# Left-over dots of the last stage in the ring's slots, and a denser, longer list of dots before it

## The chip, the cores and the metric

One core of a Trainium2 chip runs the kernel, with its engines PE (TensorE, matmuls), DVE (VectorE), ACT (ScalarE), POOL (GpSimd, which here issues the gathers) and SP (SyncE, which issues the plain loads). The metric is the device time of one execution in microseconds. Lower is better.

## The reference, cut to what matters

The layer mixes 512 tokens of width 1024 (RG-LRU and gated linear attention heads) and then sends each token through a PEER expert mixer. The change touches only the mixer:

```python
def _peer(u, w_q, keys, u_tab, v_tab):
    ...
    top_s, pos = lax.top_k(cand_s, PEER_TOPK)              # 16 of 16384 experts in each of 8 heads
    expert = jnp.take_along_axis(cand_e, pos, axis=-1)
    weight = jax.nn.softmax(top_s, axis=-1).astype(u.dtype)
    ...
    def block(args):
        xb, eb, wb = args
        act = jax.nn.gelu(jnp.einsum("td,tkd->tk", xb, u_tab[eb]), approximate=False) * wb
        return jnp.einsum("tk,tkd->td", act, v_tab[eb])
```

Each token thus needs 128 dots of its vector u with rows of `peer_u`, and a sum of 128 rows of `peer_v` weighted by the gelu of those dots.

## The kernel before

The 512 tokens are four tiles of 128: t0, t1 (gathered) and d0, d1 (dense). A gathered tile takes each of its 128 selections by an indirect DMA that brings one row of a table for each of the 128 tokens (512 KB, `gather`, L909), issued by POOL. For `peer_u` a DVE instruction multiplies the rows with the tokens' vectors and adds up along the row (a dot, `u_fin`, L923). For `peer_v` a DVE instruction adds the weighted rows to `y` (`v_row`, L976). The dense tiles multiply with the whole of both tables on PE instead, block by block of 128 rows, 128 blocks in each table.

The mixer runs in three stages.

- Scores, 402 to 910 us: `d_scores` (L1024) for blocks b = 0 to 127 of `peer_u`, loaded by SP as `ut_s` three blocks ahead into the four slots "mid". Beside it DVE makes the selections (`select`) and dots of t0, then t1. The program's order here is written by a loop (L1219 to L1233) that runs at build time over two lists, `pe_list` and `dve_list`, each with a clock made up of estimates: a block of scores counts 3.45. Whenever the second clock has reached `due`, the loop writes a dot (`row_u`), adds 1.32 to that clock and PACE to `due`. It stops when "end" is in `done`, which `pe_list` sets after block 121 (L1174). "sel" is set at block 100, once both selections of the dense tiles have been turned. The order on ACT, PE, DVE and POOL is that of the list (`manual_schedule`, L1151); nothing ties a dot to a block of scores but the slots and rows it needs.
- Middle stage, 910 to 1120 us: the loop at L1242. It builds, from one-hot products, the weights of the dense tiles into A, and adds up `peer_v` rows of t0 on PE (`v_load_pairs`, `v_pairs`). In 14 of its 32 rounds it also starts a dot of t1 (L1254). PE, ACT and DVE keep the written order (PIN); POOL's order is chosen by the scheduler.
- Last stage, 1120 to 1607 us: the loop at L1280 over the 128 blocks of `peer_v`, loaded as `vt_s` four blocks ahead into "mid". For five blocks of six `v_split` (L1067) splits weights and values into high and low parts: ACT casts `gh` and `vh`, DVE subtracts to `gl` and `vl`, and `d_out` (L1081) runs three products on PE. Every sixth block runs unsplit. Beside it `rest` (L1266) works off what t1 still needs: for each head its left-over dots, then 16 rows of `v_row`. There are n_g = left-over dots + 128 such steps, spread over 124 blocks (L1289).

Slots matter here. `ring()` gives one of four slots of 128x1024 floats (RING, L41), used in turn. Tag `u_d` has two slots, which hold the dense tiles' vectors until the scores end; then `vl` takes them in turn. A dot's rows go where `u_start` (L914) says: into the ring, into `rz` for every third dot before "sel", and into `rw`, in tag `u_d`, once "u" is set, which is after the scores. Behind the last dot of a head `u_done` (L928) runs a gelu on ACT and a product on DVE.

Of the kernel before, what the change touches and what calls it, by code (L numbers as in the profile page):

```python
# [47 lines left out]
def tile_kernel(ctx, tc, x, cx, pos, ada_w, cols, rows, consts, w_in, wgate, w_g, w_out, w_q, keys_t,  # L48
# [219 lines left out]
    def load_in(c0):  # L268
        while todo and (c0 not in ready or len(ready) < AHEAD):
            c = todo.pop(0)  # L270
            ready[c] = load_one(c)
        return ready.pop(c0)
# [25 lines left out]
    w = load_in(2464)  # L298
# [325 lines left out]
    for n, k in enumerate((0, 1, 2, 3, 4, 5, 6, 7)):  # L624
        tag, nb = (("acc", 1) if n < 1 else ("wraw", 3) if n < 4 else ("whi", 2) if n < 6 else ("wlo", 2))
        w = wst.tile([128, D], F32, name="wo", tag=tag, bufs=nb)
# [19 lines left out]
    def wq_load(a):  # L646
        wq[a] = za.tile([128, KD, 128], F32, name="wq", bufs=4)
        SY.dma_start(wq[a], w_q[a])
# [21 lines left out]
    def ring(shape=(128, D), dt=F32):  # L670
        return B.tile(list(shape), dt, name="ring", tag="ring", bufs=RING)
# [10 lines left out]
    def prep_mm(t):  # L682
        xt, pt = xin[t]
        V.tensor_add(xt, xt, pt)
        for n in range(2):
            p = bank("pw")
            for k in range(KD):
                PE.matmul(p, mix_k(k)[:, t * 128:(t + 1) * 128], wo[k][:, n * 512:(n + 1) * 512],
                          start=(k == 0), stop=(k == KD - 1))
            V.tensor_mul(pt[:, n * 512:(n + 1) * 512], p, gate_mix[:, n * 512:(n + 1) * 512])  # L690
        V.tensor_add(xt, xt, pt)
        SY.dma_start(x1_d[t * 128:(t + 1) * 128, :], xt)
        ss = kb.tile([128, 1], F32, name="ss1", bufs=2)
        S.activation(pt, xt, AF.Square, accum_out=ss)
        r = rstd_of(kb, ss, 1, 1.0 / D)
        V.tensor_scalar(pt, xt, r[:, 0:1], None, op0=OP.mult)
# [4 lines left out]
    def prep_t(t):  # L701
        pt = xin[t][1]
        ut = [tok_u(t, k) for k in range(KD)]
        for h in range(2):
            p = bank("pt")
            for j in range(4):
                PE.transpose(p[:, j * 128:(j + 1) * 128], pt[:, (h * 4 + j) * 128:(h * 4 + j + 1) * 128], ident)
            for j in range(4):
                k = h * 4 + j
                if j % 2:  # L710
                    S.activation(ut[k], p[:, j * 128:(j + 1) * 128], AF.Identity,
                                 scale=a2[:, k:k + 1], bias=b2[:, k:k + 1])
                else:
                    V.tensor_scalar(ut[k], p[:, j * 128:(j + 1) * 128], a2[:, k:k + 1], b2[:, k:k + 1],
                                    op0=OP.mult, op1=OP.add)

    def prep_n(t):
        u_n[t] = B.tile([128, D], F32, name=f"u_n{t}")
        for h in range(2):
            p = bank("pu")  # L720
            for j in range(4):
                PE.transpose(p[:, j * 128:(j + 1) * 128], tok_u(t, h * 4 + j), ident)
            S.copy(u_n[t][:, h * 512:(h + 1) * 512], p)
# [4 lines left out]
    def q_mm(ts, h):  # L728
        p = bank("pq")
        for j in range(2):  # L730
            w = wq.pop(h * 2 + j)
            for k in range(KD):
                PE.matmul(p[:, j * 256:(j + 1) * 256], w[:, k], pair_u(ts, k), start=(k == 0), stop=(k == KD - 1))
        q = zq.tile([128, 2, 2, 128], F32, name="q", bufs=2)
        S.copy(q, p.rearrange("p (j t i) -> p j t i", j=2, t=2))
        return ts, h, q

    def s_mm(ts, h, q):
        p = bank("pss")
        for i, t in enumerate(ts):  # L740
            for j in range(2):
                c = (i * 2 + j) * 128
                PE.matmul(p[:, c:c + 128], q[:, j, i], kt[:, h * 2 + j, :], start=True, stop=True)
        for i, t in enumerate(ts):
            if (t, h // 4) not in ss_:
                ss_[t, h // 4] = s_slot([128, 8, 128], "s")
            S.copy(ss_[t, h // 4][:, h % 4 * 2:h % 4 * 2 + 2],
                   p[:, i * 256:(i + 1) * 256].rearrange("p (j t) -> p j t", j=2))
            done.add((t, h))
# [105 lines left out]
    def open_l():  # L855
        za_s.close()
        wst_s.close()
        lp = pool(ctx, "lp")
        L["st"] = [lp.tile([128, 2, 128], F32, name="sel_t", tag="st", bufs=4) for _ in range(4)]
        L["z"] = [lp.tile([128, 127], F32, name=f"z{i}") for i in range(8)]  # L860
        L["lp"] = lp
        for z in L["z"]:
            G.memset(z, 0.0)
        L["ix"] = lp.tile([128, 128], I32, name="ix")
        L["at"] = lp.tile([128, 128], F32, name="at")
        L["a"] = []
        open_a(0)
# [41 lines left out]
    def gather(tab, ix, g):  # L909
        G.indirect_dma_start(out=g, out_offset=None, in_=tab,  # L910
                             in_offset=bass.IndirectOffsetOnAxis(ap=ix, axis=0))
        return g

    def u_start(t, k):  # L914
        if "u" in done:
            g = B.tile([128, D], F32, name="rw", tag="u_d", bufs=2)
        elif "sel" not in done and k % 3 == 2:
            g = zs.tile([128, D], F32, name="rz", bufs=2)
        else:
            g = ring()  # L920
        return t, k, gather(peer_u, sel_i[t][:, k:k + 1], g)
# [183 lines left out]
    def row_u():  # L1105
        g = u_next(t0) or (not left[t0]["u"] and u_next(t1))
        if g:
            u_fin(*g)
        return g

    done = set()
# [7 lines left out]
    def pe_list():  # L1119
        prep_mm(t0)  # L1120
        prep_mm(t1)
        yield 28
        prep_mm(d0)
        prep_t(t0)
        prep_t(t1)
        yield 16
        between = {1: lambda: (prep_n(t0), prep_mm(d1)), 3: lambda: prep_t(d0), 4: lambda: prep_n(t1),
                   5: lambda: prep_t(d1)}
        last = None
        for h in range(NH):  # L1130
            for a in (h * 2 + 4, h * 2 + 5):
                if a < 16:
                    wq_load(a)
            q = q_mm(GT, h)
            if last:
                s_mm(*last)
            last = q
            if h in between:
                between[h]()
            yield 22.5 if h == 1 else 8.2  # L1140
        s_mm(*last)
        open_l()
        done.add("l")
        seq = [("u", 0), ("u", 1)]
        for h in range(NH):
            seq += [("w", 2 * h), ("w", 2 * h + 1)] + [("u", 4 * h + 2 + i) for i in range(4)]
        seq += [("u", b) for b in range(34, 128)]
        for n in range(3):
            u_load(*seq[n])
        last = None  # L1150
        region.enter_context(tc.manual_schedule(engines={ET.Activation, ET.PE, ET.DVE, ET.Pool}))  # L1151
        for n, (kind, b) in enumerate(seq):
            if n + 3 < len(seq):
                u_load(*seq[n + 3])
            if kind == "w":
                if b % 2:
                    if last:
                        s_mm(*last)
                    last = q_mm(DT, b // 2)
                    yield 8.1  # L1160
                continue
            if b == A_PARTS[1]:
                open_a(1)
            if b == A_PARTS[2]:
                while not all(("turn", t) in done for t in DT):
                    yield None
                done.add("sel")
                open_a(2)
            d_scores(b)
            if last and b == 34:  # L1170
                s_mm(*last)
                last = None
            yield 3.45
            if b == 121:  # L1174
                done.add("end")
        done.add("u")
        flush(True)
        region.close()
# [31 lines left out]
        while "end" not in done:  # L1210
            yield None

    PACE = 2.4
    due = 70.
    ET = mybir.EngineType
    region = ExitStack()
    clock = [0.0, 52.0]
    streams = [pe_list(), dve_list()]
    while streams[0] or streams[1]:  # L1219
        if "l" in done and "u" not in done:  # L1220
            flush()
        if "end" not in done and clock[1] >= due and clock[1] <= clock[0] + 4 and row_u():
            clock[1] += 1.32
            due = max(due + PACE, clock[1] - 6)
            continue
        i = 0 if streams[0] and (clock[0] <= clock[1] or not streams[1]) else 1
        c = next(streams[i], "end")
        if c == "end":
            streams[i] = None
        elif c is None:  # L1230
            clock[i] = clock[1 - i] + 0.1
        else:
            clock[i] += c  # L1233
# [4 lines left out]
    with tc.manual_schedule(engines=PIN):  # L1238
# [3 lines left out]
        for n in range(0, 64, 2):  # L1242
# [8 lines left out]
            if 2 <= n:  # L1251
                if late:
                    u_fin(*late.pop())
                g = n < 30 and u_next(t1)  # L1254
# [11 lines left out]
    def rest():  # L1266
        for h in range(NH):
# [3 lines left out]
            for _ in range(TOPK):  # L1271
                v_row(t1, left[t1]["v"].pop(0))
                yield

    n_g = len(left[t1]["u"]) + NSEL
    gath = rest()
    k = 0
# [91 lines left out]
```

## Time and profile before

| | |
|---|---|
| median of 3 runs | 1616.89 us (1609.41 to 1619.64) |
| profiled execution | 1608.13 us |
| its span | 1606.4 us |
| PE busy | 1486.4 us (93%) |
| DVE busy | 1193.9 us (74%) |
| POOL busy | 630.4 us (39%) |
| ACT busy | 527.1 us (33%) |
| HBM read | 477.69 MB |
| dots in `ring`, `rz`, `rw` | 159, 63, 34 |

The span runs from the first to the last instruction of the profiled execution. Busy shares are means over stages with different limits, so the stages have to be read one by one, by windows of time. PEclk is the granted clock of PE as a share of 2.4 GHz. The DMA share is the mean busy share of the core's 16 DMA engines; it can come out just over 1.

### The profile page before, as it was taken

Reading aid. Unit: us, or ns where it says so; the run is one execution under the profiler, and the core shown is the slowest. Engines: PE = TensorE matmul, PEld = TensorE weight load, DVE = VectorE, ACT = ScalarE, POOL = GpSimd, SP = SyncE. Lnnn points to the kernel's source line nnn. Section 1 sums busy time; section 2 is a strip of 40 time slices with the busy share of each in tenths; the row PEclk is TensorE's granted clock in tenths of the full one; section 3 lists DMA queues with packets and bytes.
Section 4 is the critical chain, followed back from the end, with each engine's and each line's share of the span. In section 5 each row is a group of like instructions: output and inputs, shape, how many; then the busy total and the mean of one; then the engine's idle time right before and its main releaser. Section 6 shows DMA issues by size and latency. Waiting matters only on the chain. (4 is left out here: it accounts for less than half of the span.)

```text
span 1606.4 us, 20273 instructions
## 1 busy us (share of the span) xinstructions
PE 1486.4 (93%) x6668; PEld 1103.9 (69%) x6668; DVE 1193.9 (74%) x3078; ACT 527.1 (33%) x1001; POOL 630.4 (39%) x579
## 2 busy tenths in 40 slices
PE   8899999999999999999999999999899999696585
PEld 2678778478888888888888744454566667474354
DVE  5889965429989979997964177666788889584467
ACT  3667874122111111111120144444333443232123
POOL 0111100005546646564544376664545555241230
PEclk9999999999999999999999999999999999897798
DMA  9655432448999989998999699999899999795575
GB/s 373 199 183 177 145 118 79 185 152 296 361 359 394 388 324 405 387 399 329 394 371 395 216 347 351 358 348 356 326 359 370 386 369 390 281 332 212 175 258 214
DMA packets 152569, 484.28 MB, mean 301 GB/s; under 512 B 14864, under 2 KB 36752, under 8 KB 152336
## 3 DMA queue, kind: packets, MB, share of 16 engines
q0 software_dynamic: 79072, 287.87, 48.6%
q1 hardware_dynamic: 73392, 195.13, 32.7%
q8 instruction: 52, 0.85, 0.2%
q14 instruction: 53, 0.43, 0.1%
HBM read 477.69 MB, written 5.24 MB: 301 GB/s over the span
## 5 line engine op out<-in xcount | busy, mean ns | idle before, releaser
L910 POOL DMA_INDIRECT ring<-in_dram,sel_i x287 | 363.6, 1267 | 374.8 <-DVE y L982 150.1
L1030 PE MATMUL pds<-u_d,ut_s 128*128 128x256 f32 x2048 | 444.8, 379 | 0.0
L1030 PEld LDWEIGHTS pds<-u_d,ut_s 128*128 128x128 f32 x2048 | 388.4, 190 | 52.5
L924 DVE SCALAR_TENSOR_TENSOR ring<-ring,u_n 128x1024 f32<-128x1024 f32 x159 | 191.8, 1219 | 35.4 <-DMA ring<-in_dram,sel_i 35.3
L1090 PE MATMUL ya<-vl,gh 128*128 128x512 f32 x428 | 146.1, 424 | 63.8 <-DVE vl L1078 63.0
L982 DVE SCALAR_TENSOR_TENSOR y<-ring,act,y 128x1024 f32<-128x1024 f32 x127 | 162.5, 1280 | 28.2 <-DMA ring<-in_dram,sel_i 27.4
L1090 PE MATMUL ya<-vh,gh 128*128 128x512 f32 x428 | 147.5, 427 | 7.1 <-ACT vh L1076 7.1
L1090 PEld LDWEIGHTS ya<-vl,gh 128*128 128x128 f32 x428 | 81.5, 199 | 96.2 <-DVE vl L1078 79.3
L1090 PE MATMUL ya<-vh,gl 128*128 128x512 f32 x428 | 139.7, 409 | 0.0
L1078 DVE TENSOR_TENSOR vl<-vt_s,vh 128x1024 fp32r<-128x1024 f32 x107 | 132.7, 1240 | 9.0 <-ACT vh L1076 8.8
L1033 ACT ACTIVATE A<-pds 128x1024 f32<-128x1024 f32 x32 | 32.8, 1024 | 302.9 <-PE pds L1030 276.9
L1076 ACT CAST vh<-vt_s 128x1024 fp32r<-128x1024 f32 x107 | 112.3, 1049 | 59.3 <-DMA vt_s<-in_dram 47.0
L973 PE MATMUL yv<-ring_s,z 128*64 128x512 f32 x256 | 121.4, 603 | 5.9 <-DMA ring_s<-in_dram,ix 4.0
L973 PE MATMUL yv<-ring,z 128*64 128x512 f32 x256 | 121.5, 603 | 1.2 <-DMA ring<-in_dram,ix 0.7
L1075 ACT CAST gh<-A 128x256 fp32r<-128x256 f32 x107 | 43.4, 405 | 214.7 <-PE ya L1090 192.7
L1090 PEld LDWEIGHTS ya<-vh,gh 128*128 128x128 f32 x428 | 84.2, 198 | 36.9 <-ACT vh L1076 10.0
L910 POOL DMA_INDIRECT rz<-in_dram,sel_i x63 | 76.6, 1215 | 64.0 <-DVE rz L924 37.2
L1090 PEld LDWEIGHTS ya<-vh,gl 128*128 128x128 f32 x428 | 85.0, 199 | 21.1
L924 DVE SCALAR_TENSOR_TENSOR rw<-rw,u_n 128x1024 f32<-128x1024 f32 x34 | 41.6, 1224 | 73.5 <-DMA rw<-in_dram,sel_i 71.5
L1039 DVE TENSOR_TENSOR ab<-cst,sel_t 128x512 f32<-128x512 f32 x64 | 44.1, 689 | 58.7 <-PE pwb L1054 31.8
L910 POOL DMA_INDIRECT ring<-in_dram,ix x64 | 62.8, 982 | 47.9 <-PE pwb L1054 22.1
L910 POOL DMA_INDIRECT ring_s<-in_dram,ix x64 | 63.9, 998 | 44.4 <-DMA ut_s<-in_dram 20.8
(310 smaller groups left out, 2375.5 us busy)
## 6 DMA issues: line engine op xcount, KB each, us to landing
ut_s<-in_dram SPq DMA_DIRECT2D x144, 512.0 KB
vt_s<-in_dram SPq DMA_DIRECT2D x128, 512.0 KB
adw<-in_dram POOLq DMA_DIRECT2D x34, 512.0 KB
wraw<-in_dram SPq DMA_DIRECT2D x21, 512.0 KB
wada<-in_dram SPq DMA_DIRECT2D x16, 512.0 KB
wq<-in_dram SPq DMA_DIRECT2D x16, 512.0 KB
ring<-in_dram,sel_i POOLq DMA_INDIRECT x287
wo<-in_dram SPq DMA_DIRECT2D x8, 512.0 KB
```

The costliest lines, as they stand in the source:

```text
L910: G.indirect_dma_start(out=g, out_offset=None, in_=tab, in_offset=bass.IndirectOffsetOnAxis(ap=ix, axis=0))
L924: V.scalar_tensor_tensor(g, g, 1.0, u_n[t], op0=OP.mult, op1=OP.mult, accum_out=act[t][:, k:k + 1])
L973: PE.matmul(yv[0][h * 64:h * 64 + 64, n, :], z[:, 63 - i:127 - i], g[:, n * 512:(n + 1) * 512], start=(i == 0), stop=(i == 63), skip_group ...
L982: V.scalar_tensor_tensor(L["y"], g, a, L["y"], op0=OP.mult, op1=OP.add)
L1030: PE.matmul(p, ut[:, k], u_d[k // 4][:, k % 4].rearrange("p j t -> p (j t)"), start=(k == 0), stop=(k == KD - 1))
L1033: S.activation(a_of(b - 3, 4), ld["ps"].rearrange("p h n -> p (h n)"), AF.Gelu)
L1039: V.tensor_tensor(ab[:, 0], iota[:, None, :].to_broadcast([128, 4, 128]), st[0][:, j, n0:n0 + 4, None].to_broadcast([128, 4, 128]), op=OP. ...
L1075: S.copy(gh, a)
L1076: S.copy(vh, vt)
L1078: V.tensor_sub(vl, vt, vh.bitcast(F32))
L1090: PE.matmul(ya[t][:, n, :], g[:, j * 128:(j + 1) * 128], v[:, n * 512:(n + 1) * 512], start=(b == 0 and i == 0), stop=(b == 127 and i == l ...
```

## The change

Three edits. A dot started after the middle stage, marked by "w", takes its slot from the ring instead of `rw`. The build loop paces the dots by LATE = 2.2 instead of 2.4 once "sel" is set. "end", at which the loop writes no more dots, comes after block 124 instead of 121.

```diff
--- before.py
+++ after.py
@@ -912,7 +912,9 @@
         return g
 
     def u_start(t, k):
-        if "u" in done:
+        if "w" in done:
+            g = ring()
+        elif "u" in done:
             g = B.tile([128, D], F32, name="rw", tag="u_d", bufs=2)
         elif "sel" not in done and k % 3 == 2:
             g = zs.tile([128, D], F32, name="rz", bufs=2)
@@ -1171,7 +1173,7 @@
                 s_mm(*last)
                 last = None
             yield 3.45
-            if b == 121:
+            if b == 124:
                 done.add("end")
         done.add("u")
         flush(True)
@@ -1210,7 +1212,7 @@
         while "end" not in done:
             yield None
 
-    PACE = 2.4
+    PACE, LATE = 2.4, 2.2
     due = 70.
     ET = mybir.EngineType
     region = ExitStack()
@@ -1221,7 +1223,7 @@
             flush()
         if "end" not in done and clock[1] >= due and clock[1] <= clock[0] + 4 and row_u():
             clock[1] += 1.32
-            due = max(due + PACE, clock[1] - 6)
+            due = max(due + (LATE if "sel" in done else PACE), clock[1] - 6)
             continue
         i = 0 if streams[0] and (clock[0] <= clock[1] or not streams[1]) else 1
         c = next(streams[i], "end")
@@ -1272,6 +1274,7 @@
                 v_row(t1, left[t1]["v"].pop(0))
                 yield
 
+    done.add("w")
     n_g = len(left[t1]["u"]) + NSEL
     gath = rest()
     k = 0
```

## Rows read from the trace of the kernel before

**Rows 1.** the page, busy tenths of 40 slices of 40.16 us, granted clock, DMA share.

```profile
PE   8899999999999999999999999999899999696585
PEclk9999999999999999999999999999999999897798
DMA  9655432448999989998999699999899999795575
```

**Rows 2.** windows: length, busy us (instructions) of PE PEld DVE ACT POOL, PEclk, DMA, GB/s.

```profile
1160.00:1382.00 222.00, 212.95 (x825) 153.00 (x824) 196.90 (x207) 87.60 (x122) 110.66 (x87) 1.00 0.99 378
1382.00:1407.00 25.00, 12.40 (x35) 7.62 (x34) 9.73 (x15) 4.72 (x7) 4.61 (x4) 0.79 0.52 185
1448.50:1542.00 93.50, 54.14 (x155) 36.54 (x154) 37.81 (x56) 17.07 (x25) 16.07 (x16) 0.79 0.52 177
```

**Rows 3.** lines L1022 and L910 from 1160 to 1382; columns: ns min/median/max, first, last.

```profile
L1022 SPq DMA_DIRECT2D vt_s<-in_dram x73: 327/328/328, 1160.4 to 1381.0; - x73
...
L910 POOL DMA_INDIRECT ring<-in_dram,sel_i x87: 932/938/2014, 1159.2 to 1379.7; - x87
```

**Rows 4.** waits, 1448.5 to 1542; columns: us in total, times, longest us.

```profile
DVE rw L924 <- DMA rw<-in_dram,sel_i: 54.9, 15, 7.4
...
PE ya L1090 <- DVE vl L1078: 34.2, 10, 7.8
```

**Rows 5.** timeline of one dot; columns: start, us, instruction, idle before and releaser.

```profile
1458.50 0.94 POOL L910 DMA_INDIRECT rw<-in_dram,sel_i  x1 [6.19 <-DVE rw L924]
...
1459.81 1.22 PE L1090 MATMUL ya<-vl,gh 128*128 128x512 f32 x2 [7.79 <-DVE vl L1078]
...
1463.09 1.23 DVE L924 SCALAR_TENSOR_TENSOR rw<-rw,u_n 128x1024 f32<-128x1024 f32 x1 [3.34 <-DMA rw<-in_dram,sel_i]
```

**Rows 6.** timeline of POOL, first gathers of and after the two groups of dots.

```profile
1382.05 0.94 POOL L910 DMA_INDIRECT rw<-in_dram,sel_i  x1 [0.30 <-issue]
...
1407.02 2.01 POOL L910 DMA_INDIRECT ring<-in_dram,sel_i  x1 [9.23 <-DVE y L982]
...
1448.59 0.94 POOL L910 DMA_INDIRECT rw<-in_dram,sel_i  x1 [0.62 <-DVE vl L1078]
...
1542.37 1.86 POOL L910 DMA_INDIRECT ring<-in_dram,sel_i  x1 [9.54 <-DVE y L982]
```

**Rows 7.** the page, groups; columns: busy us, mean ns, idle before and releaser.

```profile
L982 DVE SCALAR_TENSOR_TENSOR y<-ring,act,y 128x1024 f32<-128x1024 f32 x127 | 162.5, 1280 | 28.2 <-DMA ring<-in_dram,sel_i 27.4
...
L924 DVE SCALAR_TENSOR_TENSOR rw<-rw,u_n 128x1024 f32<-128x1024 f32 x34 | 41.6, 1224 | 73.5 <-DMA rw<-in_dram,sel_i 71.5
```

**Rows 8.** lines L924 and L1030 from 808 to 910.

```profile
L924 DVE SCALAR_TENSOR_TENSOR ring<-ring,u_n x31: 1218/1225/1249, 809.1 to 876.9; 128x1024 f32<-128x1024 f32 x31
...
L1030 PE MATMUL pds<-u_d,ut_s x464: 379/379/382, 807.7 to 909.8; 128*128 128x256 f32 x155
```

**Rows 9.** timeline of DVE and POOL where the scores end.

```profile
869.56 1.92 POOL L910 DMA_INDIRECT ring<-in_dram,sel_i  x1 [1.50 <-DVE ring L924]
...
876.88 1.23 DVE L924 SCALAR_TENSOR_TENSOR ring<-ring,u_n 128x1024 f32<-128x1024 f32 x1 [0.93 <-DMA ring<-in_dram,sel_i]
...
878.38 0.93 POOL L910 DMA_INDIRECT ring<-in_dram,ix  x1 [1.24 <-DVE ring L924]
900.07 0.93 POOL L910 DMA_INDIRECT ring_s<-in_dram,ix  x1 [20.76 <-DMA ut_s<-in_dram]
...
911.25 1.00 DVE L1062 TENSOR_TENSOR A<-A,pwb 128x112 f32<-128x112 f32 x4 [33.14 <-ACT A L1033]
```

**Rows 10.** windows of the end of the scores.

```profile
880.00:910.00 30.00, 30.00 (x140) 26.21 (x138) 0.00 (x0) 2.05 (x2) 3.60 (x4) 1.00 0.56 193
```

**Rows 11.** windows of two stretches of other rate in the last stage.

```profile
1200.00:1240.00 40.00, 37.99 (x148) 27.32 (x147) 35.27 (x38) 15.88 (x22) 20.52 (x17) 1.00 0.96 364
1360.00:1380.00 20.00, 20.00 (x80) 14.57 (x79) 18.51 (x21) 8.65 (x12) 7.01 (x9) 1.00 1.02 408
```

**Rows 12.** waits, 1120 to 1607.

```profile
ACT act L932 <- DVE rw L924: 36.7, 2, 18.8
```

## The prediction

> **What bounds the kernel now.** I read the page's forty slices first. PE is near full through the kernel except in slices 35, 37, 38 and the last ones, where its digits fall to 6, 6, 5, the granted clock's digits fall with them, and so do those of the DMA engines [rows 1]. Where PE, its clock and the DMA engines all sink together, something serial stands in their way. All of it lies in the last stage, the loop over 128 value blocks (L1280), so I cut that stage into stretches [rows 2]. From 1160 to 1382 us it runs evenly: granted clock 1.00, which is the level of 2.4 GHz, and a DMA share of 0.99 at 378 GB/s. In the stretches 1382 to 1407 and 1448.5 to 1542 the DMA share is 0.52 and the granted clock 0.79, a mix of both levels.
>
> What limits the even stretch is read from its transfers: 73 loads of value blocks and 87 gathers of 512 KB each in 222 us [rows 3], that is 160 x 0.524 MB / 222 us = 378 GB/s, the whole of what the DMA engines moved there at a share of 0.99. So a transfer costs 222 / 160 = 1.3875 us, a block 222 / 73 = 3.04 us, and one gather with its share of the block loads 222 / 87 = 2.55 us.
>
> What limits the bad stretches is read from the waits of the second: DVE waits 54.9 us in 15 pieces for the gathered rows of `rw`, and PE waits 34.2 us for `vl` [rows 4]. One round shows why. `rw` takes its slot from tag u_d, which has two slots and also holds `vl`. The gather of a dot starts at 1458.50, once the dot before it has given its slot back; DVE can take the dot only at 1463.09, after 3.34 us of waiting for that transfer, and the next `vl` stands behind the dot on DVE's in-order list; PE in turn had stood 7.79 us for a `vl` [rows 5]. The gather waits for the dot before it, or for a `vl` that PE still reads, the dot for the gather, the next `vl` for the dot, and PE for that: one such round trip per dot, with only two slots to run ahead in. The first bad stretch goes from the first `rw` gather at 1382.05 to the next `ring` gather at 1407.02 (4 dots), the second from 1448.59 to 1542.37 (16 dots) [rows 6]: 25.0 + 93.8 = 118.8 us for 20 dots, 5.94 us each.
>
> **The change part by part.**
>
> (1) Left-over dots into the ring. After the middle stage `u_start` takes a ring slot, as `v_row` does, and `vl` has both u_d slots to itself. A left-over dot is then, to every queue, what a row of `v_row` is: one gather on POOL, one DVE pass over 128x1024. On DVE it is 1224 ns and a short read of the accumulator, against 1280 ns for a row of y [rows 7], so no dearer. A pace for it stands in the trace: that of the even stretch, 2.55 us. The four ring slots let gathers run ahead there: DVE waits for them only 27.4 us over 127 rows [rows 7]. The first stretch becomes 4 x 2.55 = 10.2 instead of 25.0, the second 16 x 2.55 = 40.8 instead of 93.8: −14.8 and −53.0, together **−67.8 us**. The bounds for a dot in the ring are 1.39 us (its transfer alone) and 5.94 us (no gain from the slots); I take 2.55, the row for the same gather, slots and queue. The lost clock needs no term of its own: its cost lies inside the length of the stretches.
>
> (2) More dots before the middle stage. The build loop paces dots by its own clock, 3.45 per block of d_scores. After "sel" (block 100) it went 22 blocks to "end" (block 121): 22 x 3.45 / 2.4 = 31.6, and the trace has 31 dots after the last `rz` one [rows 8]. Now it goes 25 blocks at 2.2: 25 x 3.45 / 2.2 = 39.2, so 39, eight more. The middle loop takes its 14 as before, so 12 are left over for the last stage instead of 20; n_g falls from 148 to 140, and the 12 all belong to head 7. Eight transfers fewer in a stage bound by transfers: 8 x 1.3875 = **−11.1 us**. (Bounds: nothing, if the stage were bound by PE; 8 x 2.55 = 20.4 us, if each gather cost a whole slot of the pace. The DMA share of 0.99 speaks for the transfer.)
>
> What the eight cost where they now stand: a gather each on POOL, ahead of the eight gathers for the first pairs of the middle stage, and a pass each on DVE, ahead of the products with A. The dots there are not tied to PE; their list order alone is set, and they run as fast as slots and transfers let them, 31 in 809.1 to 876.9, 2.26 us each, while PE runs its scores to 909.8 without a gap [rows 8]. So the smaller pace buys a place earlier in the list rather than a faster pass, and eight dots add 8 x 2.26 = 18.1 us to DVE's list. DVE now stands idle 33.14 us, from 878.0 to 911.25, for the last scores [rows 9]; the cover is 15 us longer than needed. On POOL the last dot's gather moves from 869.56 to 887.7 and the fourth `ring<-in_dram,ix` gather from 878.38 to 896.5; its first `ring_s` gather waits until 900.07 for a block of scores anyway [rows 9], 2.6 us later than POOL would be through. A gather in this crowded stretch needs 876.88 − 869.56 = 7.3 us from issue to use, so the pair rows are there by 904, against 910 when they are wanted. The DMA engines are 56% busy between 880 and 910 [rows 10], which leaves 13.2 us of them; eight transfers need 11.1. So it costs **0**, with little to spare on POOL and DMA. If the cover is gone, the middle stage begins up to 18.1 − 6 = 12 us late (rival D).
>
> (3) What is late next. At the end of a head ScalarE's gelu waits for the head's last dot, and the next block's `vh` cast stands behind it: that was 36.7 us of waiting at two heads [rows 12], inside the bad stretches. Head 6 now ends in the middle loop; for head 7 it stays. I take **+2 us**, between nothing and one old round trip of 5.94, nearer to nothing since `vh` has two slots.
>
> Sum: −67.8 − 11.1 + 0 + 2 = **−76.9 us**. The profiled execution took 1608.1 us around a span of 1606.4, so it would take 1531; the median of the runs is 8.8 us higher, and the same sum from it gives 1540; from the mean of the three runs (1615.3) it gives **1538**, which I take.
>
> A rule that speaks against the price of a transfer: the Trainium skill, "DMA: Bandwidth & Descriptors", section "Bandwidth", says that for transfers between HBM and SBUF the HBM side binds at about 358 GB/s per core. By that rule the 268 transfers of the new last stage would take about 21 us longer than at 378, and an estimate from it would be about 1559. The trace differs: 378 GB/s over 222 us and 408 over 20 us [rows 2, 11]; the measurement decides.
>
> **The rivals.**
>
> A. The ring doesn't run ahead at the end. If POOL's order puts each gather behind a wait for the dot before it, a dot in the ring still costs 5.94: 12 x (5.94 − 2.55) = 41 us back, 1579. If the 16 rows of head 7 behind the dots are caught too, 28 x 3.39 = 95 us, and the kernel is **slower, 1633**; it decides from 23 such gathers on (76.9 / 3.39). For it: POOL is in order, and the order there is the scheduler's. Against it: 87 gathers through the same ring in the even stretch run at 2.55 [rows 3].
>
> B. The loop doesn't give more dots (its list ends on another bound than the pace): 20 are left, the 11.1 us stay, 1549. Against it: 31.6 computed, 31 seen.
>
> C. Transfers at a lower rate. Between 1200 and 1240 they moved 364 GB/s [rows 11], 1.440 us each: 268 x 0.053 = 14 us back, 1552. The rule of the Trainium skill's page "DMA: Bandwidth & Descriptors" above would be this case taken 7 us further.
>
> D. The hand-over to the middle stage comes late: 12 us, 1550; with all 18, 1556. For it: 2.6 us of margin on POOL.
>
> E. Transfers faster. At the 408 GB/s of 1360 to 1380 [rows 11], 1.285 us each: 268 x 0.1025 = 27.5 us more gain, 1511. Against it: PE is 20.00 of 20 us busy there, so it holds only in stretches.
>
> **How the numbers follow.** Forecast 0.53; A 0.08 (12 dots 0.04 at 1579; 18 to 27 gathers 0.02, within 1%; 28 gathers 0.02, slower); B 0.07; C 0.13; D 0.11; E 0.08. Predicted: 1538. The range 1518 to 1560 takes in B, C, D and the nearer part of E (20 us of its 27.5), and leaves out A and E's far end, about 0.12. Faster by over 1% (over 16 us, about what runs of this kernel can tell from no change): forecast, B, C, D, E and A's first case, 0.96; within 1%: 0.02; slower: 0.02.
>
> **What would show it.** After the middle stage no `rw` gather; some 12 dots on `ring` in the last stage; the waits of PE for `vl` without 7 us pieces; granted clock and DMA share near 1.0 from 1160 to the end of the value blocks; some 39 dots after the last `rz`, the last near 895; PE through its scores by 910 and in the last stage by 1120 as before. Wrong would be: PE's scores ending late (D, or scores starved of loads), dots in the last stage that each wait 3 us or more for their rows (A), 20 of them (B), or an even DMA share with fewer GB/s (C).

## The result, and the profile after

The changed kernel takes 1532.14 us, median of its runs (1531.13 to 1534.27), against 1616.02 us of the kernel before beside it: a ratio of 0.9487, with a 95% interval of 0.9454 to 0.952. On a later occasion it was 1533.73 against 1614.53, ratio 0.9494 (0.9477 to 0.9511). The profiled execution went from 1608.1 to 1531.1 us and its span from 1606.4 to 1529.4, 77.0 us less; the sum had said 76.9.

The page first, busy tenths of the 40 slices (now 38.2 us each), granted clock and DMA share, of the changed kernel; compare [rows 1]:

```profile
PE   8899999999999999999999999989978999999995
PEclk9999999999999999999999999999999999999998
DMA  9665532626999999999899999999999999999995
```

The dip of all three near the end is gone. PE, its clock and the DMA engines now fall off together only in the last slice, which is the finish after the last block.

Windows of the changed kernel's last stage, the even part and the stretch in which its left-over dots stand (columns as in [rows 2]):

```profile
1160.00:1429.00 269.00, 262.13 (x1020) 190.68 (x1021) 240.19 (x254) 108.43 (x150) 136.36 (x101) 1.00 0.98 375
1429.00:1461.00 32.00, 31.47 (x124) 22.63 (x122) 27.61 (x42) 13.73 (x20) 13.92 (x12) 1.00 0.98 368
```

The stretch with the dots, 1429 to 1461, now looks like the one without them: granted clock 1.00 and a DMA share of 0.98 in both, where the stretches of before had 0.79 and 0.52. Line numbers below 914 stay; of those used here, L924 of before is now L926, L1030 is L1032, L1078 is L1080 and L1090 is L1092.

The dots by their slots (first row: the last stage; second: the whole kernel):

```profile
L926 DVE SCALAR_TENSOR_TENSOR ring<-ring,u_n x11: 1211/1216/1299, 1431.7 to 1458.3; 128x1024 f32<-128x1024 f32 x11
...
L926 DVE SCALAR_TENSOR_TENSOR rw<-rw,u_n x14: 1212/1218/1220, 925.7 to 1020.7; 128x1024 f32<-128x1024 f32 x14
```

Eleven dots are left over for the last stage, all in the ring; `rw` keeps the 14 of the middle loop. In the page's count of gathers into the ring by `sel_i`, 307 stand against 287: 11 left-over dots and 9 that moved into the scores. The 11 take 1431.7 to 1458.3, that is 26.6 us for 10 steps, 2.66 us each.

One of them in the timeline, to be held against [rows 5]:

```profile
1435.80 0.94 POOL L910 DMA_INDIRECT ring<-in_dram,sel_i  x1 [0.61 <-DVE ring L926]
1436.98 1.21 DVE L926 SCALAR_TENSOR_TENSOR ring<-ring,u_n 128x1024 f32<-128x1024 f32 x1
...
1438.87 1.23 DVE L1080 TENSOR_TENSOR vl<-vt_s,vh 128x1024 fp32r<-128x1024 f32 x1 [0.33 <-ACT vh L1078]
1440.02 1.22 DVE L926 SCALAR_TENSOR_TENSOR ring<-ring,u_n 128x1024 f32<-128x1024 f32 x1
```

The gather at 1435.80 starts as an earlier dot gives a ring slot back, and it fetches the rows of a dot several places later. The dots of 1436.98 and 1440.02 show no wait in brackets: their rows were there. Between them `vl` follows its cast at once.

Waits of the last stage, 1120 to 1530 (us in total, times, longest):

```profile
POOL ring L910 <- DVE y L984: 138.6, 93, 3.9
...
PE ya L1092 <- DVE vl L1080: 14.5, 17, 2.9
...
ACT act L934 <- DVE ring L926: 1.4, 1, 1.4
```

PE's wait for `vl` is 14.5 us in 17 pieces of at most 2.9; it was 63.0 us in 30 pieces of up to 10.5 over the whole of that stage before. The gelu at the end of the one head left waits 1.4 us instead of 36.7 for two heads [rows 12]. What POOL waits for is a free ring slot; DVE, which takes the rows, waits for rows of `y` only 20.1 us in 24 pieces in that stage, and for rows of the dots 1.0 us.

The edges of the stages, from the rows of the scores and of the last stage's products (ns min/median/max, first and last start):

```profile
L1032 PE MATMUL pds<-u_d,ut_s x2048: 379/379/382, 401.8 to 909.6; 128*128 128x256 f32 x187
...
L1092 PE MATMUL ya<-vh,gh x428: 387/389/796, 1120.5 to 1510.5; 128*128 128x512 f32 x143
```

The scores end at 909.6 (before 909.8 [rows 8]), the last stage begins at 1120.5 (before 1120.1) and the last product of this row starts at 1510.5 instead of 1587.0. All of the gain lies in the last stage.

### The profile page after: what moved, and what is told of

Its sections match the earlier page's. It is cut to its first block, busy times and chain, and to the rows that moved or that the text cites. A ratio compares the mean times of both kernels' runs of the same rounds, so it can differ in the third digit from the quotient of the medians.

```text
span 1529.4 us, 20273 instructions
## 1 busy us (share of the span) xinstructions
PE 1458.6 (95%) x6668; PEld 1092.5 (71%) x6668; DVE 1193.2 (78%) x3078; ACT 528.8 (35%) x1001; POOL 649.9 (42%) x579
## 4 chain that ended last, share of the span: by engine, by line
PE 62%; DMA 16%; DVE 8%; issue 7%; ACT 4%; POOL 2%; SPq 0%; DVEq 0%; POOLq 0%; ACTq 0%
PE pds L1032 29%; DMA ring<-in_dram,sel_i 9%; PE pq L733 7%; PE yv L975 6%; PE ya L1092 5%; PE pw L688 4%; PE pwb L1056 3%; DMA ring_s<-in_dram,ix 2%; POOL ring L910 2%; DMA vt_s<-in_dram 2%; DMA wada<-in_dram 2%; DVE y L984 1%; DMA adw<-in_dram 1%; PE pss L743 1%; DVE vl L1080 1%
## 5 line engine op out<-in xcount | busy, mean ns | idle before, releaser
L910 POOL DMA_INDIRECT ring<-in_dram,sel_i x307 | 399.2, 1300 | 382.9 <-DVE ring L926 139.0
L1032 PE MATMUL pds<-u_d,ut_s 128*128 128x256 f32 x2048 | 444.8, 379 | 0.0
L1032 PEld LDWEIGHTS pds<-u_d,ut_s 128*128 128x128 f32 x2048 | 388.4, 190 | 52.5
L926 DVE SCALAR_TENSOR_TENSOR ring<-ring,u_n 128x1024 f32<-128x1024 f32 x179 | 216.3, 1219 | 51.3 <-DMA ring<-in_dram,sel_i 51.0
L984 DVE SCALAR_TENSOR_TENSOR y<-ring,act,y 128x1024 f32<-128x1024 f32 x127 | 162.6, 1280 | 21.1 <-DMA ring<-in_dram,sel_i 20.1
L1092 PE MATMUL ya<-vl,gh 128*128 128x512 f32 x428 | 137.3, 402 | 15.0 <-DVE vl L1080 14.5
L1080 DVE TENSOR_TENSOR vl<-vt_s,vh 128x1024 fp32r<-128x1024 f32 x107 | 131.6, 1230 | 17.5 <-ACT vh L1078 16.5
L1092 PE MATMUL ya<-vh,gh 128*128 128x512 f32 x428 | 142.2, 413 | 1.5 <-ACT vh L1078 1.5
L1078 ACT CAST vh<-vt_s 128x1024 fp32r<-128x1024 f32 x107 | 112.3, 1050 | 61.7 <-DMA vt_s<-in_dram 48.1
L1092 PE MATMUL ya<-vh,gl 128*128 128x512 f32 x428 | 133.2, 392 | 0.0
L1092 PEld LDWEIGHTS ya<-vl,gh 128*128 128x128 f32 x428 | 79.2, 189 | 39.3 <-DVE vl L1080 22.2
L910 POOL DMA_INDIRECT rz<-in_dram,sel_i x63 | 76.1, 1208 | 64.4 <-DVE rz L926 37.5
L1092 PEld LDWEIGHTS ya<-vh,gh 128*128 128x128 f32 x428 | 80.5, 189 | 29.4 <-issue 9.8
L1092 PEld LDWEIGHTS ya<-vh,gl 128*128 128x128 f32 x428 | 80.6, 188 | 19.8
L1056 PEld LDWEIGHTS pwb<-ab 128*128 128x128 f32 x512 | 61.1, 191 | 31.7 <-issue 18.8
L910 POOL DMA_INDIRECT ring<-in_dram,ix x64 | 63.3, 989 | 43.9 <-PE yv L975 15.9
L910 POOL DMA_INDIRECT ring_s<-in_dram,ix x64 | 69.4, 1084 | 23.5 <-issue 15.8
```

The source lines that it names most:

```text
L910: G.indirect_dma_start(out=g, out_offset=None, in_=tab, in_offset=bass.IndirectOffsetOnAxis(ap=ix, axis=0))
L926: V.scalar_tensor_tensor(g, g, 1.0, u_n[t], op0=OP.mult, op1=OP.mult, accum_out=act[t][:, k:k + 1])
L984: V.scalar_tensor_tensor(L["y"], g, a, L["y"], op0=OP.mult, op1=OP.add)
L1032: PE.matmul(p, ut[:, k], u_d[k // 4][:, k % 4].rearrange("p j t -> p (j t)"), start=(k == 0), stop=(k == KD - 1))
L1056: PE.matmul(p[:, n * 128:(n + 1) * 128], ab[:, 1, n], ab[:, 0, n], start=True, stop=True)
L1078: S.copy(vh, vt)
```

## The experiments

Three groups of four, each on a chip of its own (10, 8 and 15), with runs of the kernel before beside it. That kernel's time differed between the groups: it took 1594.5 us (median) beside the first four experiments, 1597.6 beside the next four and 1614.5 beside the last four, so ratios are compared, or kernels of one group (more on this in the last section).

| run | what it is | median us | ratio to before (95%) |
|---|---|---|---|
| (the change) | | 1532.1 | 0.9487 (0.9454 to 0.952) |
| e_slots | slots alone, 20 left over | 1520.9 | 0.9552 (0.9518 to 0.9587) |
| e_list | list alone, dots in `rw` | 1554.8 | 0.9753 (0.9722 to 0.9784) |
| e_own1 | left-over dots in one slot of their own | 1555.9 | 0.9773 (0.9737 to 0.9809) |
| e_front | same dots, written closer and earlier | 1515.0 | 0.9503 (0.947 to 0.9535) |
| e_reuse | 16 gathers fewer | 1510.6 | 0.9467 (0.9438 to 0.9495) |
| e_nodve | 16 DVE passes fewer | 1511.3 | 0.9485 (0.9439 to 0.9532) |
| e_more | still more dots ahead | 1523.4 | 0.9548 (0.9519 to 0.9578) |
| e_end | pace 2.4, later end | 1520.4 | 0.9517 (0.9485 to 0.9549) |
| after_again | the change once more | 1533.7 | 0.9494 (0.9477 to 0.9511) |
| e_none | 16 rows fewer, gather and pass | 1526.3 | 0.9455 (0.9439 to 0.9472) |
| e_pe | 84 matmuls fewer | 1531.3 | 0.9481 (0.9463 to 0.9498) |
| e_both | both of these | 1520.2 | 0.9412 (0.9395 to 0.9429) |

**The two parts by themselves: e_slots and e_list.** Diffs against the changed kernel.

```diff
-            if b == 124:
+            if b == 121:
...
-    PACE, LATE = 2.4, 2.2
+    PACE, LATE = 2.4, 2.4
```

> The slots alone: left-over dots in the ring, pace 2.4 and the end after block 121 as before, so 20 dots are left over. Theory (a dot in the ring costs what a row of v_row costs): 67.8 us of the gain come from the slots, and the 20 dots stay as 20 transfers; with 9 dots more than in the changed kernel (which leaves 11) at 1.39 us each, 1532 + 12.5 = 1545 us. Rival (a dot keeps its round trip of 5.94 us wherever its rows go, and the gain came from there being fewer of them): above 1600 us.

Measured: ratio 0.9552, 71.4 us less than the 1594.5 beside it (interval 65.8 to 76.9 us). The prediction's terms for the slots and for the gelu, −67.8 and +2, make 65.8. Its rival is off by far more than the interval. The slots carry most of the gain.

```diff
-    done.add("w")
```

> The list alone: pace 2.2 and the end after block 124, but the left-over dots stay in rw, in the two slots of vl; 11 are left over instead of 20. Theory (each dot in rw costs a round trip of 5.94 us): 9 x 5.94 = 53 us less than before, 1563 us, with stretches in the last stage where PE waits 7 us for vl. Rival (the list saves only a transfer per dot, 1.39 us): 1604 us.

Measured: ratio 0.9753, 39.4 us less for nine dots, 4.4 us each. That lies between the two expectations, and the first was reckoned wrongly: it took the whole round of 5.94 us for a dot that goes away, but the blocks that PE works on within that round have still to be done. By the prediction's own terms a dot that leaves `rw` for good saves the round less the even pace, 3.39, and a transfer, 1.39, together 4.78, or 43 us for nine. The bad stretch is still there for the other eleven; waits of e_list in its last stage, 1120 to 1560:

```profile
DVE rw L926 <- DMA rw<-in_dram,sel_i: 41.1, 11, 5.0
...
PE ya L1092 <- DVE vl L1080: 28.5, 19, 6.2
```

Eleven waits for the rows of `rw`, 3.7 us each, and PE behind `vl` for 28.5 us. Each part alone takes 71 and 39 us away, both together 82 by the ratio of the change (0.0513 x 1594.5): they treat the same dots, so they don't add up. Behind the slots the list is worth (0.9552 − 0.9494) x 1614.5 = 9 us.

**What in the two slots cost: e_own1.**

```diff
         if "w" in done:
-            g = ring()
+            g = L["own"].tile([128, D], F32, name="own", tag="own", bufs=1)
...
     done.add("w")
+    L["own"] = pool(ctx, "own")
```

> The changed kernel, but the 11 left-over dots take one slot of their own, which vl never uses and no other gather either. Theory (what costs is that the next gather cannot start before the dot before it has ended): a round trip per dot as before, 11 x (5.94 - 2.55) = 37 us on top, 1569 us. Rival (what cost was that dots and vl shared the two slots): as the changed kernel, 1532 to 1536 us.

Measured: ratio 0.9773, and 41 us above e_front of the same group, which has the changed kernel's slots and ten left-over dots. The round trip is enough: `vl` has both u_d slots to itself here, and the kernel is as slow as e_list, where the same dots are in `rw`. Timeline of two dots of e_own1:

```profile
1423.50 0.94 POOL L910 DMA_INDIRECT own<-in_dram,sel_i  x1 [9.95 <-DVE own L926]
...
1427.98 1.23 DVE L926 SCALAR_TENSOR_TENSOR own<-own,u_n 128x1024 f32<-128x1024 f32 x1 [3.22 <-DMA own<-in_dram,sel_i]
...
1429.48 0.94 POOL L910 DMA_INDIRECT own<-in_dram,sel_i  x1 [5.04 <-DVE own L926]
...
1434.05 1.23 DVE L926 SCALAR_TENSOR_TENSOR own<-own,u_n 128x1024 f32<-128x1024 f32 x1 [3.31 <-DMA own<-in_dram,sel_i]
...
1436.87 1.22 PE L1092 MATMUL ya<-vl,gh 128*128 128x512 f32 x2 [3.03 <-DVE vl L1080]
```

The gather starts at 1423.50 as the dot before it ends, its rows come 3.2 to 3.3 us after DVE has begun to wait, the dot runs at 1427.98, the next gather at 1429.48, the next dot at 1434.05: one dot in 6.07 us, and PE waits for the `vl` that DVE makes after it. One slot of its own is as bad as two shared ones; the four of the ring let the gathers run ahead. That the sharing with `vl` does no harm does not follow, for this run has one slot less as well. In e_list, with two slots shared, DVE takes its dots so:

```profile
1446.18 1.23 DVE L926 SCALAR_TENSOR_TENSOR rw<-rw,u_n 128x1024 f32<-128x1024 f32 x1 [3.41 <-DMA rw<-in_dram,sel_i]
...
1447.67 1.27 DVE L1080 TENSOR_TENSOR vl<-vt_s,vh 128x1024 fp32r<-128x1024 f32 x1
...
1452.36 1.22 DVE L926 SCALAR_TENSOR_TENSOR rw<-rw,u_n 128x1024 f32<-128x1024 f32 x1 [3.42 <-DMA rw<-in_dram,sel_i]
...
1455.68 1.23 DVE L926 SCALAR_TENSOR_TENSOR rw<-rw,u_n 128x1024 f32<-128x1024 f32 x1 [2.09 <-DMA rw<-in_dram,sel_i]
```

With a `vl` between two dots the next dot comes 6.18 us after the one before; with none between, 3.32 us. So it may be that `vl` takes up the second slot and leaves one to the dots. Two slots without `vl`, and how many would just do, were not tried.

**Whether the written pace is a pace: e_front.**

```diff
-            if b == 124:
+            if b == 115:
...
-    PACE, LATE = 2.4, 2.2
+    PACE, LATE = 2.4, 1.4
```

> The changed kernel with the same dots (41 instead of 40) written at a pace of 1.4 up to block 115, so all of them stand earlier and closer in the list. Theory (nothing ties a dot to a block of scores, transfers set their pace): spacing of the dots after the last rz 2.1 to 2.4 us as with pace 2.2, scores end near 910 us, 1532 us within 4. Rival (the written pace is the pace on the chip): the dots come 1.4 us apart, the loads of the scores are starved and the scores end later; over 1540 us.

Measured: ratio 0.9503, no difference from the changed kernel within the intervals. First and last dot on DVE after the last `rz`, of e_front, 41 dots:

```profile
814.48 1.23 DVE L926 SCALAR_TENSOR_TENSOR ring<-ring,u_n 128x1024 f32<-128x1024 f32 x1 [1.00 <-DMA ring<-in_dram,sel_i]
...
906.33 1.23 DVE L926 SCALAR_TENSOR_TENSOR ring<-ring,u_n 128x1024 f32<-128x1024 f32 x1 [0.84 <-DMA ring<-in_dram,sel_i]
```

and of the changed kernel, 40 dots:

```profile
810.56 1.22 DVE L926 SCALAR_TENSOR_TENSOR ring<-ring,u_n 128x1024 f32<-128x1024 f32 x1 [1.16 <-DMA ring<-in_dram,sel_i]
...
900.20 1.23 DVE L926 SCALAR_TENSOR_TENSOR ring<-ring,u_n 128x1024 f32<-128x1024 f32 x1
```

91.85 us for 40 steps, 2.30 us; and 89.64 us for 39 steps, 2.30 us. The list says 1.4 in one and 2.2 in the other; the pace is the same. Windows from 810 to 900, of e_front and of the changed kernel:

```profile
810.00:900.00 90.00, 90.00 (x428) 79.42 (x427) 53.94 (x97) 12.52 (x29) 44.46 (x39) 1.00 0.99 373
```

```profile
810.00:900.00 90.00, 90.00 (x428) 79.44 (x427) 53.66 (x97) 13.57 (x30) 39.25 (x38) 1.00 0.99 372
```

The DMA share is 0.99 in both, and DVE is busy 54 us of 90: the dots come at the pace of their transfers. The edit of the pace changes how many dots stand ahead of the middle stage in the list, and no other effect of it shows here.

**How much cover is left: e_more and e_end.**

```diff
-            if b == 124:
+            if b == 127:
...
-    PACE, LATE = 2.4, 2.2
+    PACE, LATE = 2.4, 2.0
```

> Pace 2.0 after the selections and the end only after block 127: 53 dots after the last rz instead of 40, none left over for the last stage. Theory (the cover at the end of the scores is used up): the last stage loses 11 transfers, 15 us, but 13 dots more at 2.26 us put DVE's list 29 us later, to 925 us, where it is wanted from 911, and the transfers of that stretch have no room left; the middle stage comes 10 to 20 us late, 1527 to 1540 us. Rival (there was more cover than reckoned): 1517 us.

Measured: ratio 0.9548; two dots are left over after all. The middle stage comes late: in e_more it takes 210.6 us from the last score (912.1) to the first product of the last stage (1122.7), in e_end of the same group 194.8. PE where the middle stage begins, and the window around it, of e_more:

```profile
929.26 1.08 PE L975 MATMUL yv<-ring,z 128*64 128x512 f32 x1 [16.76 <-DMA ring<-in_dram,ix]
...
910.00:930.00 20.00, 3.24 (x14) 2.27 (x14) 10.87 (x21) 1.24 (x2) 14.46 (x13) 0.67 0.90 331
```

The same window of e_end:

```profile
910.00:930.00 20.00, 20.00 (x105) 11.54 (x105) 10.27 (x32) 8.10 (x25) 13.55 (x14) 1.00 0.83 294
```

PE stands 16.76 us for the first gathered pair rows, since POOL has issued the dots' gathers first; its clock is granted at 0.67 in that window, against 1.00. The last stage of e_more is the shorter for it, 1122.7 to 1499.5 = 376.8 us against 394.0 in e_end, but the cover was used up, and the kernel is slower than the changed one by ratio (0.9548 against 0.9494).

```diff
-    PACE, LATE = 2.4, 2.2
+    PACE, LATE = 2.4, 2.4
```

> The changed kernel with pace 2.4, only the end after block 124: 37 dots after the last rz, 14 left over instead of 11. Theory (each dot moved ahead saves a transfer of 1.39 us): 1532 + 4 = 1536 us. Rival (dots ahead of the middle stage are not free): 1532 us or less.

Measured: ratio 0.9517, which by 0.9494 is 4 us more than the change, as the theory said; but the intervals overlap, so this run alone settles nothing.

**What bounds the last stage: e_reuse and e_nodve.** In `v_row`, first a gather less, then a pass less:

```diff
-        g = gather(peer_v, sel_i[t][:, k:k + 1], ring())
+        if k % 8 == 7:
+            g = fin["row"]
+        else:
+            g = fin["row"] = gather(peer_v, sel_i[t][:, k:k + 1], ring())
```

> The changed kernel without 16 of the 128 gathers of peer_v rows for t1: every eighth row of y is added from the rows of the selection before it, so part of y is other data; DVE does all its passes. Theory (the last stage is bound by transfers at 1.39 us each): 16 x 1.39 = 22 us less, 1510 us. Rivals: DVE or PE bounds the stage: 1532 us; a gather costs its whole slot of the pace, 2.55 us: 1491 us.

Measured: ratio 0.9467. Against 0.9494 of the change that is 4 us, uncertain by 5, where transfers as the only bound would have given 22 (a ratio near 0.936, outside the interval). The theory fell.

```diff
         g = gather(peer_v, sel_i[t][:, k:k + 1], ring())
...
+        if k % 8 == 7:
+            return
```

> The changed kernel with all its gathers, but without the DVE pass for every eighth of t1's peer_v rows (these 16 rows are left out of y). Theory (bound by transfers): 1532 us, at most 3 us less. Rival (DVE, 91% busy there, bounds the stage): 16 x 1.28 = 20 us less, 1512 us.

Measured: ratio 0.9485, no difference within 8 us: the 20 us of the rival (a ratio near 0.937) lie outside the interval, so DVE, busy 89% of the even stretch, does not bound the stage by itself either.

**Two bounds at once: e_none, e_pe, e_both, beside after_again.** `e_none` returns before the gather of every eighth row; `e_pe` cuts the third product in every sixth block; `e_both` does both.

```diff
+        if k % 8 == 7:
+            return
         g = gather(peer_v, sel_i[t][:, k:k + 1], ring())
...
         prods = ((p[0], p[1]),) if len(p) == 2 else ((p[0], p[2]), (p[0], p[3]), (p[1], p[2]))
+        if b % 6 == 2:
+            prods = prods[:2]
```

> The changed kernel itself, for a comparison on one chip with the next three: a ratio of 0.949 to the kernel before, as first measured.

> The changed kernel without every eighth of t1's peer_v rows at all: 16 gathers and 16 DVE passes fewer, these rows are left out of y. Theory (the last stage is bound by transfers): 22 us less than the changed kernel. Rival that e_reuse and e_nodve brought up (PE is the bound, at 2.79 us for a split block and 3.03 us for an unsplit one, 362 us in all, and the transfers stand just behind it): 3 to 6 us less. Rival (DVE and transfers together, either alone being enough to hold the pace): 15 to 20 us less.

> The changed kernel without the third product (low part of the weights by high part of the values) in every sixth block, which leaves that term out of y for those blocks: 21 x 4 matmuls of 0.2325 us, 19.5 us fewer on PE; every transfer and every DVE pass stays. Theory (bound by transfers): 0 to 3 us less than the changed kernel. Rival (bound by PE): 15 to 20 us less. Rival (PE and transfers about level): 5 to 10 us less.

> Both: no row of every eighth peer_v selection of t1, and no third product in every sixth block. Theory (bound by transfers): 22 us less than the changed kernel, as without the rows alone. Rival (bound by PE): 15 to 20 us less, as without the product alone. Rival (level): 18 to 24 us less, more than the two of them give alone when added up.

Measured, in us of 1614.5 below after_again: e_none 6.3, e_pe 2.1, e_both 13.2, each with some 4 us of uncertainty. Neither the transfers alone (22 expected) nor PE alone (15 to 20) is the bound; the case "level" fits best, though 2.1 is less than the 5 to 10 it gave for e_pe, 13.2 is less than the 18 it gave for e_both, and that it is more than the sum of the two, 8.4, is not beyond the uncertainty. Windows from 1160 to 1440 of after_again, e_none, e_pe and e_both, one after the other (columns as in [rows 2]):

```profile
1160.00:1440.00 280.00, 274.69 (x1068) 199.22 (x1067) 250.50 (x266) 113.41 (x158) 146.17 (x107) 1.00 0.98 376
```

```profile
1160.00:1440.00 280.00, 278.11 (x1093) 204.66 (x1092) 240.17 (x261) 116.61 (x161) 121.98 (x95) 1.00 0.96 357
```

```profile
1160.00:1440.00 280.00, 266.94 (x1007) 189.33 (x1006) 249.68 (x266) 111.06 (x157) 151.93 (x107) 0.99 0.99 377
```

```profile
1160.00:1440.00 280.00, 273.17 (x1048) 194.97 (x1047) 244.10 (x270) 115.31 (x164) 133.85 (x98) 1.00 0.98 367
```

After_again has both near full: PE busy 274.69 of 280 us, DMA share 0.98. Without the 16 rows the rate falls to 357 GB/s and the share to 0.96, and PE fills to 278.11. With less for PE to do, PE falls to 266.94 and the transfers stay at 377 GB/s and 0.99. Whichever of the two is relieved, little is gained, and the other stays near full.

That does not make the two the whole of the bound. As an estimate from the rows, PE's products need 362 us by the prices in the expectation of e_none, and the 267 transfers of the stage 267 x 1.3875 = 370 us; from its first product to its last the stage took 389.0 us in after_again. For e_both the same estimate gives 343 and 348 us, and the stage took 375.8. Some 20 to 30 us are left that neither price accounts for, and what holds them is not shown.

## Why the prediction was right

The time, 1532.1, lies within 1518 to 1560, and 6 us below the 1538 given. The sum against the profiled execution was right almost to the digit, 1531.2 against 1531.1. To that digit it was luck: the slots and the list, as measured below, are 2 to 6 us off their terms, in opposite directions. What differed was the step from it to a median: the runs of before spread over 10 us above their profiled execution, those of the changed kernel over 3 us.

Point by point:

- **The diagnosis** (a round trip per dot, on two slots shared with `vl`) held in its first half: e_own1 shows that the round trip costs, with nothing shared. What the sharing with `vl` adds to it was not separated.
- **Slots**, −67.8 with +2 for the gelu: e_slots measured −71.4 (65.8 to 76.9). The 2.55 us taken for a dot in the ring were 2.66.
- **The list**, −11.1: about −9 behind the slots (0.9552 to 0.9494, uncertain by some 6 us), and the last stage went from 397.1 us in e_slots to 390.0 in the changed kernel, though in other groups. The count was off by one: 40 dots after the last `rz` and 11 left over, where 39 and 12 were forecast. The reason given for the size was too simple. The step read the DMA share of 0.99 as the only bound and priced a gather at its transfer, though PE was busy 212.95 of 222 us in the same row [rows 2]; e_reuse, e_none and e_both show that the transfers are not the only bound, and a gathered row less is worth 0.4 us there, not 1.39. Yet a left-over dot less is worth about what was forecast: on one chip the last stage went from 394.0 us with 14 left over (e_end) to 376.8 with 2 (e_more), 1.43 us each, and on another from 397.1 with 20 (e_slots) to 386.3 with 10 (e_front), 1.08 us each, one profile of each run. A dot must then cost something that a row does not. The second head's end, which falls out of the last stage, can be a part of it (the gelu waits 6.6 us in e_slots, 1.4 in the changed kernel), but not between e_end and e_more, where the gelu waits 1.1 us in all in e_end. That was not taken apart and stays open: the size was right, the reason given for it is not shown.
- **The cover** for nine dots more in the scores held: the middle stage takes 210.9 us from the last score to the last stage's first product, against 210.3. It was nearly used up, as reckoned; the last of these dots ran at 900.2, where 895 was forecast. In the window from 880 to 910 of the changed kernel:

```profile
880.00:910.00 30.00, 30.00 (x141) 26.14 (x141) 11.67 (x21) 2.28 (x4) 13.29 (x14) 1.00 0.93 343
```

the DMA share has gone from 0.56 [rows 10] to 0.93, with PE's scores still without a gap (30.00 us of 30.00). E_more shows rival D where more is asked of it: 16 us late.

- **The rivals.** A (the ring doesn't run ahead) is excluded by the dots' 2.66 us. B (no more dots) by their count. C and E (another rate): the even part moved 375 GB/s against 378. D did not happen here. The rule of the Trainium skill, page "DMA: Bandwidth & Descriptors", section "Bandwidth", that for transfers between HBM and SBUF the HBM side binds at about 358 GB/s, is not borne out by this last stage of a kernel on one core: 375 GB/s over 269 us.

## What to carry to other kernels

A gather whose slot comes free only when the consumer of the one before has finished costs a full round trip each, 6 us here, and an in-order engine hands that wait to everything behind it; the cure here was a ring of four slots, in which several gathers are in flight. A pace written into a list is no pace on the chip when nothing ties the two engines together: ask only what stands before what, and whether the cover there still holds it. When two resources are both at 98%, don't price a saving by one of them alone; relieve each, and then both.

## What the runs showed of the hardware that was not expected

The middle stage, with the same code in it, ran at two rates in different groups of runs. Windows from 950 to 1100 of the changed kernel, beside which the kernel before took 1616 us, and of e_end, beside which it took 1598:

```profile
950.00:1100.00 150.00, 139.06 (x714) 69.35 (x712) 103.73 (x317) 68.96 (x231) 101.59 (x101) 1.00 0.96 350
```

```profile
950.00:1100.00 150.00, 148.71 (x778) 74.52 (x776) 110.75 (x339) 77.40 (x245) 107.50 (x109) 1.00 1.00 379
```

350 GB/s at a DMA share of 0.96 in the one, 379 at 1.00 in the other; the stage takes 210.9 us there and 194.8 here. The 16 us between them are about as much as the 17 to 22 us between the medians of the kernel before, which was itself profiled only at the lower rate. In that window it was 348 to 352 GB/s in the profiles of the kernel before, of the change (both times), e_none, e_pe and e_both, and 376 to 386 in all eight of the first two groups, while the last stage from 1160 to 1440 moved 373 to 380 GB/s at either rate in the runs with all their gathers and none of them in `rw` or `own`. The first two groups ran on chips 10 and 8, the third on chip 15 (for the first runs of the two kernels the chip is not on record). So the rate goes with the chip, or with the time at which it ran; what sets it was not tried.
